# Later conditioning sections of a hybrid decoder layer: from steps in the mixer to bursts in w_o, in the second norm and in the FFN

## The chip, the core and the metric

The kernel runs on one core of one Trainium2 chip. The metric is the device time of one execution in microseconds (us); all times here are in that unit. Inputs and outputs lie in the chip's HBM in float32.

## The reference

One layer of a conditioned decoder is computed for a prompt of 256 tokens and for 8 sampled sequences of 8 tokens, 320 tokens in all, with a model width of 2048. What matters of it:

```python
mod = jax.nn.silu(c) @ w_ada + b_ada            # 9 conditioning vectors, w_ada 2048 x 12288
sh1, sc1, g1, sh2, sc2, g2 = split(mod, 6)      # sections 0 to 5, 2048 columns each
h = _rmsnorm(x, norm1_g) * (1 + sc1) + sh1
p = h @ w_in                                    # q, k, v, og, u, ga, gb, low-rank gate
y_a = norm(gated linear attention(q, k, v, state)) * silu(og)
y_b = causal pooling of u, then w_pool
x = x + g1 * ((sigmoid(ga) * y_a + sigmoid(gb) * y_b) @ w_o)
h2 = _rmsnorm(x, norm2_g) * (1 + sc2) + sh2
gate, up = split(h2 @ w_gu)                     # 2048 x 11264
x = x + g2 * ((silu(gate) * up) @ w_down)       # 5632 x 2048
y = _rmsnorm(x, final_norm_g)
```

Sections 0 and 1 of `mod` are needed at the start, section 2 (`g1`) behind the product with w_o, sections 3 and 4 (`sh2`, `sc2`) for the second norm, section 5 (`g2`) behind the product with w_down. `mod` depends on the conditioning vectors alone, so each section can be computed at any time before its use.

## The kernel before

Everything is kept transposed: a row tile is 128 of the 2048 channels by 320 tokens, and there are KT = 16 of them. A product with a weight matrix is made in units of 256 output columns (`proj`). A unit is cut into chunks of four row tiles of the weight. For each chunk a block of 128 x 4 x 256 floats, 512 KB, is loaded by SyncE's DMA queue (SP) into one of three `raw` buffers (L139). ScalarE and VectorE split it into a high and a low part, `whi` (L149) and `wlo` (L150), of which five pairs are kept. TensorE makes three matmuls for each row tile and each 128 columns (L163 to L165): 24 matmuls to a chunk, 4 chunks to a unit of a product over 2048 channels. Two PSUM buffers (`pmain`) hold the sums of such units, four smaller ones (`pmisc`) everything else.

The stages in order: the head (norms, sections 0 and 1, the first attention head's projections, to about 290 us), the mixer (attention and pooling steps of four heads, interleaved by a queue of steps with the projections of heads 1 to 3), w_o (8 units, 32 chunks), the second norm, and the FFN in two halves of 22 column tiles, each first w_gu and then w_down.

Sections 2 to 5 of `mod` are made in 16 groups of 512 columns (four row tiles of `mod`). A group needs the 16 row tiles of w_ada, 128 x 512 each. Before the change, `ada_step` (L245) does four row tiles of a group: it takes two blocks of 512 KB from a pool `ap` with AB = 3 buffers, makes 16 matmuls (L215) of the small conditioning matrix `scT` with 128 x 128 pieces of w_ada, four at a time on four column strips of the array, and asks for later blocks. Each matmul in float32 shows as two records in the profile. With the fourth step of a group, ScalarE copies the sum from PSUM (L264), TensorE transposes it (L126), and VectorE adds the bias and, for sections 1 and 4, the norm's factor (L229 to L232).

What says when a step is taken is a rate: `proj` and `projs` call `ada_pump` at the end of each chunk (L177, L191), and `ada_rate` sets how many steps come to a unit: 1.4 in the mixer (L954), 1.6 in w_o (L1004), 1.0 in the FFN (L1047). The order of the sections is 4, 2, 3, 5. Whatever of the first 48 steps is left over is done before the sixth unit of w_o is read out (L1007).

Behind a unit of w_o, `residual` (L995 to L1000) multiplies by section 2 and adds to `x1`, which holds the layer's input, loaded again from a spill in HBM (L984, 16 loads at the start of the stage). `sq_acc` collects the squares for the second norm, and GpSimd forms `xs` from the sampled tokens with section 4 (L1014). The norm then sums over channels with one matmul (`rstd_bcast`, L1022), takes root and reciprocal, and forms `h2h` and `h2l` for each row tile (L1033 to L1042), on which the FFN's matmuls wait.

The order of instructions on each engine is not that of the code. A planner orders them by the time at which its own model has each one ready, with the code's order as priority; then each engine, and SP's queue, works in order. `keep_in_program_order` pins an instruction behind the one traced before it on its engine. It is used for the first of the four matmuls of each row tile of w_ada (L217), and for loads in the head alone. Memory is given out by pools on a stack: `mix` (pools `gp` and `lp`) is closed at L980, and `fp` and `f2`, opened after it, take its place, so their first writes wait for the last reads there.

Of the kernel before, what the change touches and what calls it, by code (L numbers as in the profile page):

```python
# [11 lines left out]
F32 = mybir.dt.float32  # L12
F32R = mybir.dt.float32r
I32 = mybir.dt.int32
AF = mybir.ActivationFunctionType
# [65 lines left out]
def body(tc, A):  # L81
# [42 lines left out]
    def tr(out, in_):  # L124
        k = in_.shape[0]
        PE.transpose(out, in_, ident[:k, :k])  # L126
# [5 lines left out]
    def raw_chunk(src, nk, nn, pool=None, tag="raw", bufs=3):  # L132

        if pool is None and more:
            more.reverse()
            if more[0] is not None:
                pool, bufs = more[0], 2
        t = (pool or wp).tile([P, nk, nn], F32, tag=tag, bufs=bufs, name=nm("raw"))
        ins = nc.sync.dma_start(t, src)  # L139
        if in_order[0]:  # L140
            tc.keep_in_program_order(ins)
        return t
# [24 lines left out]
    def proj(w, col, k0, k1, xh, xl):  # L167

        ps = pmain.tile([P, 2, 512], F32, tag="pm", name=nm("ps"))
        for c0 in range(k0, k1, 4):  # L170
            nk = min(4, k1 - c0)
            for j, whi, wlo in split_chunk(w[:, c0:c0 + nk, col:col + 256], nk, 256):
                kt = c0 + j
                for i in range(2):
                    mm3(ps[:, i, :T], whi[:, i * P:(i + 1) * P], wlo[:, i * P:(i + 1) * P],
                        xh[kt], xl[kt], kt == k0, kt == k1 - 1)
            ada_pump()  # L177
        return ps

    def projs(wcols, k0, k1, xh, xl):  # L180

        pp = [pmain.tile([P, 2, 512], F32, tag="pm", name=nm("ps")) for _ in wcols]
        for c0 in range(k0, k1, 4):
            nk = min(4, k1 - c0)
            for ps, (w, col) in zip(pp, wcols):
                for j, whi, wlo in split_chunk(w[:, c0:c0 + nk, col:col + 256], nk, 256):
                    kt = c0 + j
                    for i in range(2):
                        mm3(ps[:, i, :T], whi[:, i * P:(i + 1) * P], wlo[:, i * P:(i + 1) * P],
                            xh[kt], xl[kt], kt == k0, kt == k1 - 1)  # L190
                ada_pump()  # L191
        return pp

    def proj_pair(w, col, k0, k1, xh, xl):
# [17 lines left out]
    def ada_mm(ps, k, raws, w):  # L212

        for j in range(4):
            ins = PE.matmul(ps[32 * j:32 * j + 32, 0:w], lhsT=scT[:, k, :], rhs=raws[j], start=k == 0,  # L215
                            stop=k == KT - 1, tile_position=(0, 32 * j))
            if j == 0:  # L217
                tc.keep_in_program_order(ins)

# [15 lines left out]
    ada_raw = {}  # L235
    ada_ps = []

    def ada_load(c):

        if c < 8 * len(ada_q) and c not in ada_raw:  # L240
            sec, b = ada_q[c // 8]
            col = (sec * KT + b) * P
            ada_raw[c] = raw_chunk(wada[:, 2 * (c % 8):2 * (c % 8) + 2, col:col + 512], 2, 512, apool[0], "araw", AB)

    def ada_step():  # L245

        n = len(ada_done)
        sec, b = ada_q[n // 4]
        r = n % 4
        ada_done.append(n)  # L250
        for c in range(2 * n, 2 * n + 2):
            ada_load(c)
        if r == 0:
            ada_ps[:] = [misc()]
        ps = ada_ps[0]
        for j in range(4):
            raw = ada_raw[2 * n + j // 2]
            ada_mm(ps, 4 * r + j, [raw[:, j % 2, i * P:(i + 1) * P] for i in range(4)], P)
        for c in range(2 * n + 2, 2 * n + 2 + AB):
            ada_load(c)  # L260
        if r < 3:
            return
        sb = apool[0].tile([P, P], F32, tag="adasb", name=nm("adasb"))
        S.copy(sb, ps[:, 0:P])  # L264
        pt = misc()
        tr(pt[:, 0:P], sb)
        blk = sec * KT + b
        ada_out(mod[:, blk:blk + 4, :], pt[:, 0:P].rearrange("p (m c r) -> p m c r", m=4, c=1)[:, :, :, 0:9], blk, (4, 1))

    ada_done = []  # L270
    ada_acc = [0.0, 0.0, 0]

    def ada_rate(rate, limit):

        ada_acc[:] = [0.0, rate / 4, limit]

    def ada_pump():
        ada_acc[0] += ada_acc[1]
        if ada_acc[0] >= 1.0 and len(ada_done) < ada_acc[2]:
            ada_acc[0] -= 1.0  # L280
            ada_step()

    def modp(sec, kt):
        return mod[:, sec * KT + kt, 0:1]
# [4 lines left out]
    def s3(ap):  # L289
        return ap.rearrange("p (b t) -> p b t", t=LS)  # L290
# [81 lines left out]
    with tc.tile_pool(name="head", bufs=1) as xp:  # L372
# [29 lines left out]
        class HeadJob:  # L402
# [14 lines left out]
            def burst(self, k0):  # L417
                for ahead in range(3):
                    self.load(k0 + ahead * self.nk)
                raws = self.raws[k0]  # L420
                self.raws[k0] = None
                if self.ps is None:
                    self.ps = misc()
                w = self.w
                for i in range(self.nk):
                    ada_mm(self.ps, k0 + i, [raws[j // 2][:, i, (j % 2) * w:(j % 2) * w + w] for j in range(4)], w)

            def finish(self):
                nb = self.s // 2
# [138 lines left out]
                    e += 1  # L568

    in_order[0] = False  # L570
    apool = [acx.enter_context(tc.tile_pool(name="ap", bufs=1, side="right"))]


    lp = mix.enter_context(tc.tile_pool(name="lp", bufs=1))
# [405 lines left out]
    mix.close()  # L980
    fp = ctx.enter_context(tc.tile_pool(name="fp", bufs=1))
    x1 = [fp.tile([P, T], F32, name="x1_%d" % k) for k in range(KT)]
    for k in range(KT):
        nc.sync.dma_start(x1[k], xspill[k])  # L984
    acc = fp.tile([P, T], F32, tag="acc", name="acc1")

    def sq_acc(acc, k, first):
# [13 lines left out]

    xs = fp.tile([P, KT, TS], F32, name="xs")
    tiny = fp.tile([P, 1], F32, name="tiny")
    ada_rate(1.6, 48)  # L1004
    for ui in range(8):
        ps = proj(wo, 256 * ui, 0, KT, mh, ml)
        if ui == 5:  # L1007
            while len(ada_done) < 48:
                ada_step()
        for i in range(2):  # L1010
            residual(ps, i, 2 * ui + i, 2)
            k = 2 * ui + i
            sq_acc(acc, k, k == 0)
            G.tensor_tensor(s3(xs[:, k]), s3(x1[k][:, TP:T]), mods(4, k), op=ALU.mult)  # L1014
        if ui == 4:
            ada_rate(0, 0)
        if ui == 6:
            S.activation(tiny, epst, AF.Sqrt)

    def rstd_bcast(acc):  # L1020
        pt = misc()
# [3 lines left out]
        V.reciprocal(rs, rs)  # L1025
        return rs

    f2 = ctx.enter_context(tc.tile_pool(name="f2", bufs=1))
    more[:] = [f2, None]
    rs = rstd_bcast(acc)  # L1030
    h2h = [hp.tile([P, T], F32R, tag="hh%d" % k, name="h2h%d" % k) for k in range(KT)]
    h2l = [hp.tile([P, T], F32R, tag="hl%d" % k, name="h2l%d" % k) for k in range(KT)]
    for k in range(KT):  # L1033
        t = f2.tile([P, T], F32, tag="h2", bufs=3, name=nm("h2"))
# [4 lines left out]
        S.copy(h2h[k][:, TP:T], t[:, TP:T])  # L1039
# [4 lines left out]

    acc2 = fp.tile([P, T], F32, tag="acc", name="acc2")
    parts = ((0, 22), (22, 44))
    ada_rate(1.0, 64)  # L1047
    for pi, (f0, f1) in enumerate(parts):
        ah, al = {}, {}
        for f in range(f0, f1, 2):  # L1050
            sg = f2.tile([P, 2, T], F32, tag="sg", name=nm("sg"))
            if f == 0:
                pg, pu = projs(((wgu, f * P), (wgu, FF + f * P)), 0, KT, h2h, h2l)
                S.activation(sg, pg[:, :, 0:T], AF.Silu)
            else:
                pg = proj(wgu, f * P, 0, KT, h2h, h2l)
                S.activation(sg, pg[:, :, 0:T], AF.Silu)
                pu = proj(wgu, FF + f * P, 0, KT, h2h, h2l)
            V.tensor_tensor(sg, pu[:, :, 0:T], sg, op=ALU.mult)
            th = f2.tile([P, 2, T], F32R, tag="ah%d" % ((f - f0) // 2), name=nm("ah"))  # L1060
            tl = f2.tile([P, 2, T], F32R, tag="al%d" % ((f - f0) // 2), name=nm("al"))
            hilo(th, tl, sg)
            for j in range(2):
                ah[f + j], al[f + j] = th[:, j], tl[:, j]
# [68 lines left out]
```

## Time and profile before

| what | us |
|---|---|
| median of 3 runs | 2017.34 (2016.09 to 2018.74) |
| profiled execution, its own time | 2013.89 |
| its span, first to last instruction | 2012.1 |
| TensorE (PE) busy | 1958.5 |
| VectorE (DVE) busy | 1015.4 |
| ScalarE (ACT) busy | 819.7 |

The profile is of one execution. Engines: PE is TensorE's matmuls, PEld its weight loads, DVE VectorE, ACT ScalarE, POOL GpSimd, SP SyncE, which here only issues DMAs. "L215" is a line of the kernel. A row of a timeline has the start, the time taken, engine, line, operation, output<-input, shapes and the count; in brackets stands how long the engine had been idle and what released it. Matmuls overlap, so that the distance of their starts, and not the time each one takes, tells what they cost. The clock is the share of full speed that TensorE was granted. The DMA share is that of the busy time of 16 DMA engines; it can come out a little above 1 where packets overlap.

### The profile page before, as it was taken

What the parts mean: (1) busy time and instruction counts of PE and PEld (TensorE: products, weight loads), DVE (VectorE), ACT (ScalarE), POOL (GpSimd) and SP (SyncE); (2) the same over time, 40 slices, a digit from 0 to 9 for tenths busy, and PEclk for the clock granted to TensorE, in tenths of its full rate; (3) what the DMA queues carried; (4) which work ended last, traced back from release to release, by engine and by line L of the source; (5) the groups of instructions that cost most, each with busy time, mean ns of one, the idle gap of its engine ahead of it and who ended that gap; (6) DMA issues with size and microseconds to landing.
All of it is one profiled execution on the core that took longest, in us unless ns stands there. A gap on an engine that the chain in (4) does not pass through costs nothing.

```text
span 2012.1 us, 37187 instructions
## 1 busy us (share of the span) xinstructions
PE 1958.5 (97%) x15008; PEld 1851.2 (92%) x15008; DVE 1015.4 (50%) x1881; ACT 819.7 (41%) x1466; POOL 140.0 (7%) x261
## 2 busy tenths in 40 slices
PE   7999999999999999999989999999999999999997
PEld 5889998888898899888979999999999999999997
DVE  2556665465546433665574344444444444444554
ACT  4333374354335333643344333333333343444443
POOL 1112220111001100110020000000000000000000
PEclk9999999999999999999989999999999999999998
DMA  8888755776975887569736666544444554454442
GB/s 292 287 297 272 232 158 152 251 246 193 311 242 157 275 270 229 159 222 353 233 106 217 210 201 205 172 147 150 150 152 148 153 152 147 149 155 143 150 143 90
DMA packets 319598, 400.83 MB, mean 199 GB/s; under 512 B 13529, under 2 KB 259801, under 8 KB 319089
## 3 DMA queue, kind: packets, MB, share of 16 engines
q1 hardware_dynamic: 307154, 358.21, 56.1%
q0 software_dynamic: 12272, 40.25, 5.6%
q8 instruction: 117, 1.92, 0.4%
q14 instruction: 55, 0.45, 0.1%
HBM read 373.96 MB, written 24.67 MB: 198 GB/s over the span
## 4 chain that ended last, share of the span: by engine, by line
PE 92%; DMA 4%; DVE 1%; ACT 1%; issue 1%; SPq 0%; POOL 0%; ACTq 0%; POOLq 0%; DVEq 0%
PE ps L163 27%; PE ps L164 27%; PE ps L165 27%; PE pm L215 4%; DMA raw<-w_in 2%; PE pm L126 2%; DMA raw<-w_ada 2%; PE pm L797 1%; PE pm L766 1%; PE pm L818 1%; DVE wlo L150 1%; DMA xn<-x_sample 1%; PE pm L793 0%; PE pm L755 0%; PE pm L638 0%
## 5 line engine op out<-in xcount | busy, mean ns | idle before, releaser
L150 DVE TENSOR_TENSOR wlo<-raw,whi 128x512 fp32r<-128x512 f32 x952 | 659.4, 697 | 836.1 <-ACT whi L149 825.9
L149 ACT CAST whi<-raw 128x512 fp32r<-128x512 f32 x952 | 586.8, 621 | 1016.3 <-PE ps L164 868.6
L163 PE MATMUL ps<-hh,whi 128*128 128x320 f32 x1408 | 445.9, 317 | 6.9 <-ACT whi L149 2.8
L163 PE MATMUL ps<-h2h,whi 128*128 128x320 f32 x1408 | 437.6, 311 | 5.1 <-ACT h2h L1039 5.1
L165 PE MATMUL ps<-hh,wlo 128*128 128x320 f32 x1408 | 442.3, 314 | 0.3
L164 PE MATMUL ps<-hl,whi 128*128 128x320 f32 x1408 | 440.7, 313 | 0.4 <-DVE hl L492 0.4
L164 PE MATMUL ps<-h2l,whi 128*128 128x320 f32 x1408 | 435.2, 309 | 0.0
L165 PE MATMUL ps<-h2h,wlo 128*128 128x320 f32 x1408 | 435.2, 309 | 0.0
L163 PEld LDWEIGHTS ps<-hh,whi 128*128 128x128 f32 x1408 | 266.8, 190 | 30.2 <-issue 15.3
L165 PEld LDWEIGHTS ps<-hh,wlo 128*128 128x128 f32 x1408 | 266.9, 190 | 8.4 <-issue 5.7
L163 PEld LDWEIGHTS ps<-h2h,whi 128*128 128x128 f32 x1408 | 265.3, 189 | 9.3 <-ACT h2h L1039 6.1
L164 PEld LDWEIGHTS ps<-hl,whi 128*128 128x128 f32 x1408 | 266.9, 190 | 7.1 <-issue 5.4
L164 PEld LDWEIGHTS ps<-h2l,whi 128*128 128x128 f32 x1408 | 265.3, 188 | 0.0
L165 PEld LDWEIGHTS ps<-h2h,wlo 128*128 128x128 f32 x1408 | 265.2, 188 | 0.0
L163 PE MATMUL ps<-ah,whi 128*128 128x320 f32 x704 | 217.7, 309 | 0.0
L165 PE MATMUL ps<-ah,wlo 128*128 128x320 f32 x704 | 216.5, 308 | 0.0
L164 PE MATMUL ps<-al,whi 128*128 128x320 f32 x704 | 216.5, 308 | 0.0
L164 PEld LDWEIGHTS ps<-al,whi 128*128 128x128 f32 x704 | 132.0, 187 | 0.0
L163 PEld LDWEIGHTS ps<-ah,whi 128*128 128x128 f32 x704 | 132.0, 187 | 0.0
L165 PEld LDWEIGHTS ps<-ah,wlo 128*128 128x128 f32 x704 | 131.9, 187 | 0.0
L215 PE MATMUL pm<-raw,scT 128*32 128x128 f32 (+1 forms) x2688 | 110.6, 297 | 8.1 <-DMA raw<-w_ada 8.1
L215 PEld LDWEIGHTS pm<-raw,scT 128*32 128x32 f32 x2688 | 69.9, 111 | 35.9 <-issue 20.2
(279 smaller groups left out, 1539.6 us busy)
## 6 DMA issues: line engine op xcount, KB each, us to landing
raw<-w_ada SPq DMA_DIRECT2D x192, 512.0 KB, 6.0
raw<-w_gu SPq DMA_DIRECT2D x176, 512.0 KB, 3.6
raw<-w_in SPq DMA_DIRECT2D x173, 512.0 KB, 4.2
raw<-w_down SPq DMA_DIRECT2D x80, 512.0 KB, 3.4
S<-state_gla POOLq DMA_DIRECT2D x16, 1024.0 KB, 8.4
o_gs<-S POOLq DMA_DIRECT2D x16, 1024.0 KB, 5.7
raw<-w_o SPq DMA_DIRECT2D x32, 512.0 KB, 4.8
raw<-w_down SPq DMA_DIRECT2D x16, 256.0 KB, 2.6
```

The source lines that it names most:

```text
L126: PE.transpose(out, in_, ident[:k, :k])
L149: S.copy(hi, raw)
L150: V.tensor_sub(lo, raw, hi.bitcast(F32))
L163: PE.matmul(ps, lhsT=whi, rhs=xhi, start=start, stop=False)
L164: PE.matmul(ps, lhsT=whi, rhs=xlo, start=False, stop=False)
L165: PE.matmul(ps, lhsT=wlo, rhs=xhi, start=False, stop=stop)
L215: ins = PE.matmul(ps[32 * j:32 * j + 32, 0:w], lhsT=scT[:, k, :], rhs=raws[j], start=k == 0, stop=k == KT - 1, tile_position=(0, 32 * j))
L766: PE.matmul(pt, lhsT=E["kdn"][:, s, d * P:(d + 1) * P], rhs=E["vn"][:, s], start=s == 0, stop=s == 1)
L797: PE.matmul(pt[32 * j:32 * j + 32, :], lhsT=qeP[:, d, 4 * gg + j, :], rhs=E["S0", gg, d][:, j], start=False, stop=d == 1, tile_position=(0 ...
L818: PE.matmul(pt, lhsT=kpz[:, gg, j, d * P:(d + 1) * P], rhs=E["vp"][:, gg], start=True, stop=True)
```

## The change

The rate is gone. A group is now an object: `load` fetches one of its four pieces (four row tiles of w_ada, 1 MB), `burst` makes the matmuls of whole pieces, with the last piece first, and `finish` does the copy, the transpose and the bias as before. Groups 0 to 11 (sections 2, 4 and 3 in turns) are made in w_o, each in one burst of 64 matmuls over all 16 row tiles behind the chunks named in BURSTS. Group 12 comes after the last unit of w_o, group 13 after the norm's sum; both are finished in the FFN at chunk 4. Groups 14 and 15 are made in the FFN in halves, behind chunks 16, 28, 40 and 52, with two buffers in `ap`. No such matmul is left in the mixer, and the pool `ap` of the mixer is gone.

In w_o a pool `ad` has 8 buffers of 1 MB, two groups. Each tick (the end of a chunk) asks for two loads of `x1`, one or two pieces, and reads out what is ready: a unit's `residual` waits until its group of section 2 is made, and `xs` until its group of section 4 is. The buffers `h2`, `sg` and the second set of `raw` move from `f2` to `fp`, and `f2` is opened after `ad` is closed.

```diff
-AB = 3
+AB = {"ad": 8, "ap": 2}
+BURSTS = (5, 7, 9, 12, 14, 16, 19, 21, 23, 26, 28, 30)
...
-    ada_q = [(s, b) for s in (4, 2, 3, 5) for b in range(0, KT, 4)]
...
-    def ada_step():
...
+        def load(self, p, pool):
+            col = (self.sec * KT + self.b) * P
+            self.raws[p] = raw_chunk(wada[:, 4 * p:4 * p + 4, col:col + 512], 4, 512, pool, "araw", AB[pool.name])
+
+        def burst(self, p0, p1):
+            first, last = self.ps is None, p1 == 4
+            if first:
+                self.ps = misc()
+            for p in reversed(range(p0, p1)):
+                raw = self.raws.pop(p)
+                for k in range(4):
+                    ada_mm(self.ps, 4 * p + k, [raw[:, k, i * P:(i + 1) * P] for i in range(4)], P,
+                           first and p == p1 - 1 and k == 0, last and p == p0 and k == 3)
...
-    ada_rate(1.4, 48)
     for h in range(1, H):
...
-    for k in range(KT):
-        nc.sync.dma_start(x1[k], xspill[k])
...
+    ad = adx.enter_context(tc.tile_pool(name="ad", bufs=1))
+    groups = [AdaGroup(sec, 4 * b) for sec, b in ((2, 0), (4, 0), (2, 1), (3, 0), (4, 1), (2, 2), (3, 1), (4, 2), (2, 3),
+                                                  (3, 2), (4, 3), (3, 3), (5, 0), (5, 1), (5, 2), (5, 3))]
+    nbulk = len(BURSTS) + 2
...
+    def settle():
+        while pending and have(2, 2 * pending[0][1]):
+            wo_evac(*pending.pop(0))
+        for k in [k for k in late_xs if have(4, k)]:
+            late_xs.remove(k)
+            G.tensor_tensor(s3(xs[:, k]), s3(x1[k][:, TP:T]), mods(4, k), op=ALU.mult)
+
+    def load_pieces(n):
+        for _ in range(n):
+            q = st_wo["piece"]
+            if q < 4 * nbulk and q // 4 < st_wo["burst"] + 2:
+                groups[q // 4].load(q % 4, ad)
+                st_wo["piece"] += 1
+
+    def wo_tick():
+        c = st_wo["chunk"]
+        st_wo["chunk"] += 1
+        x1_load(2)
+        n = st_wo["burst"]
+        if n < len(BURSTS) and BURSTS[n] == c:
+            groups[n].burst(0, 4)
+            st_wo["burst"] += 1
+            groups[n].finish()
+        load_pieces(1 if c < 4 else 2)
+        settle()
...
     for ui in range(8):
         ps = proj(wo, 256 * ui, 0, KT, mh, ml)
...
+        pending.append((ps, ui))
+        settle()
+    tick[0] = None
+    while st_wo["piece"] < 4 * nbulk:
+        groups[st_wo["piece"] // 4].load(st_wo["piece"] % 4, ad)
+        st_wo["piece"] += 1
+    groups[nbulk - 2].burst(0, 4)
...
+    more[:] = [fp, None]
+    rs = rstd_bcast(acc)
+    groups[nbulk - 1].burst(0, 4)
+    adx.close()
     f2 = ctx.enter_context(tc.tile_pool(name="f2", bufs=1))
...
-    ada_rate(1.0, 64)
+    def ff_tick():
...
+        if c in (16, 28, 40, 52):
+            j = (c - 16) // 12
+            g = groups[nbulk + j // 2]
+            g.burst(2 * (j % 2), 2 * (j % 2) + 2)
```

More of the change, by code (lines that the diff above doesn't have):

```diff
@@ L210, in body, with ada_mm @@
     wdn = A["w_down"][0].rearrange("(kt p) n -> p kt n", p=P)
-    def ada_mm(ps, k, raws, w):
+    def ada_mm(ps, k, raws, w, start, stop):
         for j in range(4):
-            ins = PE.matmul(ps[32 * j:32 * j + 32, 0:w], lhsT=scT[:, k, :], rhs=raws[j], start=k == 0,
-                            stop=k == KT - 1, tile_position=(0, 32 * j))
+            ins = PE.matmul(ps[32 * j:32 * j + 32, 0:w], lhsT=scT[:, k, :], rhs=raws[j], start=start,
+                            stop=stop, tile_position=(0, 32 * j))
             if j == 0:
@@ L270, in body, with __init__, finish @@
[L270 to L281, printed above, removed]
+    class AdaGroup:
+        def __init__(self, sec, b):
+            self.sec, self.b, self.ps, self.raws = sec, b, None, {}
+        def load(self, p, pool):
[10 more added lines that the diff above has]
+                           first and p == p1 - 1 and k == 0, last and p == p0 and k == 3)
+        def finish(self):
+            sb = fp.tile([P, P], F32, tag="adasb", name=nm("adasb"))
+            S.copy(sb, self.ps[:, 0:P])
+            pt = misc()
+            tr(pt[:, 0:P], sb)
+            blk = self.sec * KT + self.b
+            ada_out(mod[:, blk:blk + 4, :], pt[:, 0:P].rearrange("p (m c r) -> p m c r", m=4, c=1)[:, :, :, 0:9],
+                    blk, (4, 1))
@@ L283, in modp, with chunk_done @@
+    tick = [None]
+    def chunk_done():
+        if tick[0] is not None:
+            tick[0]()
     def modp(sec, kt):
@@ L1003, in body, with have @@
     tiny = fp.tile([P, 1], F32, name="tiny")
-    ada_rate(1.6, 48)
+    adx = ExitStack()
+    ad = adx.enter_context(tc.tile_pool(name="ad", bufs=1))
+    groups = [AdaGroup(sec, 4 * b) for sec, b in ((2, 0), (4, 0), (2, 1), (3, 0), (4, 1), (2, 2), (3, 1), (4, 2), (2, 3),
+                                                  (3, 2), (4, 3), (3, 3), (5, 0), (5, 1), (5, 2), (5, 3))]
+    nbulk = len(BURSTS) + 2
+    st_wo = dict(chunk=0, piece=0, burst=0)
+    pending = []
+    late_xs = []
+    def have(sec, b):
+        return any(g.sec == sec and g.b == b - b % 4 for g in groups[:st_wo["burst"]])
@@ new lines, in x1_load, with wo_evac @@
+    def x1_load(n):
+        for _ in range(n):
+            if st_x1:
+                k = st_x1.pop(0)
+                nc.sync.dma_start(x1[k], xspill[k])
+    def wo_evac(ps, ui):
+        for i in range(2):
+            k = 2 * ui + i
+            residual(ps, i, k, 2)
+            sq_acc(acc, k, k == 0)
+            late_xs.append(k)
+        if ui == 6:
+            S.activation(tiny, epst, AF.Sqrt)
+    def settle():
[4 more added lines that the diff above has]
+            G.tensor_tensor(s3(xs[:, k]), s3(x1[k][:, TP:T]), mods(4, k), op=ALU.mult)
@@ new lines, in load_pieces @@
+    def load_pieces(n):
+        for _ in range(n):
+            q = st_wo["piece"]
[13 more added lines that the diff above has]
+        settle()
@@ L1005, in body @@
+    st_x1 = list(range(KT))
+    x1_load(4)
+    tick[0] = wo_tick
     for ui in range(8):
         ps = proj(wo, 256 * ui, 0, KT, mh, ml)
[L1007 to L1016, printed above, removed]
@@ L1046, in body @@
     parts = ((0, 22), (22, 44))
-    ada_rate(1.0, 64)
+    st_ff = dict(chunk=0)
+    def ff_tick():
+        c = st_ff["chunk"]
+        st_ff["chunk"] += 1
+        if c == 4:
+            for g in groups[nbulk - 2:nbulk]:
+                g.finish()
+            for p in range(2):
+                groups[nbulk].load(p, ap)
+        if c in (16, 28, 40, 52):
+            j = (c - 16) // 12
+            g = groups[nbulk + j // 2]
+            g.burst(2 * (j % 2), 2 * (j % 2) + 2)
+            if j < 3:
+                for p in range(2):
+                    groups[nbulk + (j + 1) // 2].load(2 * ((j + 1) % 2) + p, ap)
+            if j % 2:
+                g.finish()
+    tick[0] = ff_tick
     for pi, (f0, f1) in enumerate(parts):
@@ L1050, in body @@
         for f in range(f0, f1, 2):
[L1051 removed]
+            sg = fp.tile([P, 2, T], F32, tag="sg", name=nm("sg"))
             if f == 0:
```

44 lines of the change are left out of this document (6 added, 38 removed).

## The prediction

> **What bounds the kernel now.** First the page: the span, the engines' totals, and the shares of the chain of work that ended last.
>
> ```profile
> span 2012.1 us, 37187 instructions
> ...
> PE 1958.5 (97%) x15008; PEld 1851.2 (92%) x15008; DVE 1015.4 (50%) x1881; ACT 819.7 (41%) x1466; POOL 140.0 (7%) x261
> ...
> PE 92%; DMA 4%; DVE 1%; ACT 1%; issue 1%; SPq 0%; POOL 0%; ACTq 0%; POOLq 0%; DVEq 0%
> ```
>
> TensorE bounds the kernel over the whole, and transfers take 4% of the chain. But that is an average, so next come the stages, by the view of busy time per window: mixer, w_o, the second norm, the first 10 us of the FFN, the rest of the FFN that holds conditioning. After the window and its length stand the busy times of PE, PEld, DVE, ACT and POOL with counts, the granted clock, the DMA share, GB/s.
>
> ```profile
> 290.00:901.00 611.00, 598.22 (x4866) 538.89 (x4868) 330.18 (x663) 267.87 (x510) 64.24 (x101) 0.99 0.70 224
> 901.00:1030.00 129.00, 128.41 (x1119) 121.31 (x1111) 69.62 (x146) 47.77 (x88) 5.01 (x14) 1.00 0.81 265
> 1030.00:1040.00 10.00, 1.77 (x3) 0.87 (x4) 7.12 (x15) 2.99 (x8) 3.08 (x9) 0.58 0.18 55
> 1040.00:1050.00 10.00, 10.00 (x53) 10.00 (x53) 9.98 (x27) 7.25 (x21) 7.89 (x18) 0.74 0.17 51
> 1050.00:1290.00 240.00, 240.00 (x2019) 233.70 (x2018) 106.06 (x164) 93.47 (x158) 4.86 (x9) 1.00 0.65 202
> ```
>
> PE is idle for 12.8 us of the mixer's 611, and the DMA engines there move 224 GB/s. w_o is already the densest long stage for transfers (265 GB/s), although it carries only a quarter of the moved conditioning. That is where I look for the answer: the change makes PE's work cheaper but crowds almost all later w_ada bytes into the shortest stage.
>
> The same windows for the conditioning matmuls alone (PE, PEld):
>
> ```profile
> 290.00:901.00 611.00, 44.23 (x1196) 30.45 (x1200) 0.99 0.70 224
> 901.00:1030.00 129.00, 13.01 (x348) 8.17 (x340) 1.00 0.81 265
> 1050.00:1290.00 240.00, 17.30 (x512) 13.00 (x512) 1.00 0.65 202
> ```
>
> A step is 16 matmuls, recorded as 32. So 1196 / 32 = 37 of the 64 steps lie in the mixer, 11 in w_o (a few records are missing), 16 in the FFN.
>
> **What a step costs PE.** The timeline of PE at the end of w_o and around one step in the FFN, and from the chain a step of 32 records and half a step of 16:
>
> ```profile
> 1023.82 0.31 PE L165 MATMUL ps<-mh,wlo 128*128 128x320 f32 x1
> ...
> 1029.10 0.31 PE L165 MATMUL ps<-mh,wlo 128*128 128x320 f32 x1
> ...
> 1071.49 0.31 PE L165 MATMUL ps<-h2h,wlo 128*128 128x320 f32 x1
> 1071.73 1.08 PE L215 MATMUL pm<-raw,scT 128*32 128x128 f32 x32
> 1072.74 0.41 PE L163 MATMUL ps<-h2h,whi 128*128 128x320 f32 x1
> 1072.99 0.31 PE L164 MATMUL ps<-h2l,whi 128*128 128x320 f32 x1
> ```
> ```profile
> 422.24 1.01 PE pm L215 x32
> ...
> 529.76 0.57 PE pm L215 x16
> ```
>
> The large matmuls start 0.147 us apart (36 intervals from 1023.82 to 1029.10). From 1071.49 to 1072.99 are 1.50 us where two such intervals would take 0.29, so a step costs 1.2 us. Sixteen more records cost 1.01 - 0.57 = 0.44 us, the rest is the price of going in and out. A burst of 128 records is then 1.01 + 6 x 0.44 + 0.2 = 3.85 us against 4 x 1.2 = 4.8; half a burst is 1.01 + 2 x 0.44 + 0.2 = 2.1.
>
> **Term 1, the mixer: -58 us.** 37 steps x 1.2 = 45. To this come waits of PE for w_ada, from the view of waits (total, times, longest):
>
> ```profile
> PE pm L215 <- DMA raw<-w_ada: 8.1, 5, 3.1
> ```
>
> 8 us, nearly all in the mixer, about 2 us at half clock behind the longest waits, and some nine transposes of a finished group with edges, 3 us together. Bounds: the steps plus all 12.8 us of idle PE plus the missing 1% of clock (6 us) give -64. If half the waits move on to w_in or the attention steps and the clock gains nothing, it is -52. The PSUM buffer that each group held while it grew is inside these bounds. ACT and DVE are busy for about half of this stage, so they can follow a denser PE.
>
> **Term 2, the FFN: -11 us.** 16 steps x 1.2 = 19.2 become four half bursts, 8.4. Their loads lie beside a stage at 202 GB/s and cost nothing; the cover would have to rise by more than half to be gone.
>
> **Term 3, w_o and the second norm: +80 us.** Now this stage runs from its first matmul to the first one of the FFN:
>
> ```profile
> 901.24 0.42 PE L163 MATMUL ps<-mh,whi 128*128 128x320 f32 x1
> ...
> 1039.63 0.90 PE L163 MATMUL ps<-h2h,whi 128*128 128x320 f32 x2 [5.13 <-ACT h2h L1039]
> ```
>
> That is 138.4 us. By PE alone the new stage is 32 chunks x 24 matmuls x 0.147 = 113 us and 12 bursts x 3.85 = 46, so 159 and the norm. But what must land first? Sizes from the list of DMA issues:
>
> ```profile
> raw<-w_ada SPq DMA_DIRECT2D x192, 512.0 KB, 6.0
> ...
> raw<-w_o SPq DMA_DIRECT2D x32, 512.0 KB, 4.8
> ...
> x<-xspill SPq DMA_DIRECT2D x16, 160.0 KB, 4.8
> ```
>
> A group is 8 loads of 512 KB, 4.19 MB (now 4 pieces of 1 MB). Twelve groups and the two of the norm are 58.7 MB. When can they start? The piece buffers lie where the mixer's buffers lay, and the new pool waits for the old ones. SP's timeline, then DVE's:
>
> ```profile
> 886.44 11.14 SPq L139 DMA_DIRECT2D raw<-w_o  x3
> ...
> 901.96 1.40 SPq L139 DMA_DIRECT2D raw<-w_o  x1
> ...
> 914.60 0.42 SPq L139 DMA_DIRECT2D raw<-w_o  x1
> 915.11 2.09 SPq L984 DMA_DIRECT2D x<-xspill  x4
> ```
> ```profile
> 911.95 0.49 DVE L933 TENSOR_TENSOR mg<-EQK,mg 128x320 f32<-128x320 f32 x1
> ...
> 913.36 1.30 DVE L297 TENSOR_TENSOR ml<-mg,mh 128x320 fp32r<-128x320 f32 x3
> ```
>
> The first load into that space left 0.5 us behind the last read of the mixer's buffers, 14 us after w_o had begun (the `ml` of three row tiles, from `merged`). The attention buffers, under the pieces, are last read by the merge at 911.95, so I take 13 us for the pieces. By then 7 of 32 w_o chunks are loaded; 25 remain, 13.1 MB, and x1, 2.6 MB. Together 74.4 MB. The rate, from busy windows:
>
> ```profile
> 105.00:115.00 10.00, 9.64 (x64) 9.08 (x63) 9.93 (x24) 5.73 (x13) 7.46 (x16) 1.00 1.06 399
> 513.00:525.00 12.00, 9.88 (x122) 8.95 (x112) 9.91 (x19) 2.49 (x4) 0.53 (x2) 1.00 1.03 375
> 905.00:955.00 50.00, 50.00 (x483) 44.90 (x482) 26.68 (x60) 17.04 (x33) 2.24 (x4) 1.00 1.05 356
> ```
>
> With the engines full (share above 1.0) they moved 356 to 399 GB/s. The rows do not tell what each window's mixture was; the last one is a w_o stage with w_ada and x1, as the new one will be, but with less w_ada. I take 380, nearest to the middle row. Then 74.4 / 0.380 = 196 us. The stage is 13 + 196 + 2 (landing) + 4 (the last burst) = 215, and 4 us for holes in the stream make 219: 219 - 138.4 = +80. The 16 us that bursts save on PE, and the norm's gap in which two of them lie, are worth nothing in a stage that waits for bytes. At 399 GB/s without holes it is 205 us (+67), at 356 with 10 us of holes 238 (+100).
>
> Waits that the change adds: a burst waits for its fourth piece, and behind it on PE stand its transpose and the next w_o chunks; the pieces of group n+2 wait on SP for burst n, and the next w_o loads stand behind them; `residual` waits for its group of section 2, and with two PSUM buffers for w_o the third unit waits for burst 0. In a stream that stays full these waits cost nothing more, since group n+1 (11 us of transfer) is still under way while burst n runs. `x1` and `xs` are needed no earlier than before.
>
> The Trainium skill, DMA: Bandwidth & Descriptors, section Bandwidth, has 425 GB/s for 16 MB on a lone core, and about 358 GB/s per core where both of a pair stream. By 425 the transfers would take an estimated 175 us and the kernel 2005, by 358 an estimated 208 and 2038. The 399 of this trace, with one core at work, speaks against a cap of 358; no window reaches 425, so neither figure has a chance of its own.
>
> **Term 4, the clock: -2 us.** After the norm's gap the large matmuls start 0.267 us apart:
>
> ```profile
> 1040.87 0.47 PE L163 MATMUL ps<-h2h,whi 128*128 128x320 f32 x1
> 1041.13 0.47 PE L164 MATMUL ps<-h2l,whi 128*128 128x320 f32 x1
> ```
>
> The window 1040 to 1050 holds 53 matmuls where 68 fit: 2.2 us that a burst right before may save. Bounds 0 and -2.5.
>
> **Sum.** -58 - 11 + 80 - 2 = +9 on the profiled execution, which took 2013.89 us around its span of 2012.1. The median of the runs shown, 2017.34, is 3.45 above it, so 2013.9 + 9 + 3.4 = **2026 us**.
>
> **The rivals.** *Pieces come early.* If the new buffers come free one by one, the first eight pieces (8.4 MB, 22 us of transfer) can ride on the mixer's last 25 us, which have room:
>
> ```profile
> 880.00:890.00 10.00, 10.00 (x70) 8.82 (x68) 6.36 (x16) 6.59 (x14) 0.56 (x1) 1.00 0.39 132
> 890.00:900.00 10.00, 10.00 (x72) 9.37 (x74) 10.00 (x18) 5.26 (x11) 2.67 (x2) 1.00 0.60 205
> ```
> ```profile
> 900.12 0.80 POOL L822 DMA_DIRECT2D o_gs<-S  x1 [1.50 <-DVE S L820]
> ```
>
> The stage loses some 20 us: +9 - 20 = -11, 2006 us. It decides for faster from about 13 us of earlier start. For it: the last state left its buffer at 900.12. Against it: x1 left all together behind the last read. *The high rate.* 399 GB/s, no holes, the mixer at -60: -60 - 11 + 67 - 2 = -6, 2011; with 390 GB/s 2016. So it straddles no change. *Holes.* If SP's order makes w_o loads stand behind pieces that wait for a burst while nothing else is under way, each of the 12 rounds leaves the engines empty for about 2 us, half a burst: +24 on top, 2050. For it: one queue, in order, for all loads. Against it: two groups of buffers. *The change does not do what it says:* only the first matmul of each row tile is pinned behind its predecessors, so the planner may split bursts; 36 edges more at 0.33 us are 12 us of PE, hidden in a stage that waits for transfers. It stays within the forecast.
>
> **Chances and range.** Forecast (2018 to 2034) 0.43; early pieces 0.19; high rate 0.20; holes (2034 to 2055) 0.18. A measurement of this kernel tells about 0.2%, 4 us, from no change. Faster: 0.19 and half of 0.20, less a little, 0.28. Same: 0.11 of the high rate and 0.08 of the forecast's lower end, 0.19. Slower: 0.35 of the forecast and 0.18, 0.53. The range, **2006 to 2044**, leaves out half of the early pieces and the upper half of the holes; the forecast alone has 2018 to 2034.
>
> **What would show it.** In the profile after, the mixer should be about 555 us at some 190 GB/s with no conditioning matmuls. w_o and the norm should take 205 to 235 us with a DMA share near 1.0 and 370 to 390 GB/s, and PE should wait there for raw<-w_ada or for casts that wait for raw<-w_o. The first piece should leave within 2 us of the last merge. The FFN to the end should be about 11 to 13 us shorter. Wrong would be the step on the transfers if the share in w_o stays below 0.9 while PE is full, or if pieces leave before the last merge; wrong would be term 1 if the mixer shrinks by less than 52 us.

## The result and the profile after

The changed kernel took 2029.54 us (median of 4 runs, 2028.82 to 2030.01), the kernel before, on the same chip, 2016.71 (4 runs, 2014.64 to 2018.74). The ratio is 1.0063 with an interval of 1.0046 to 1.0081: slower by 0.6%. The forecast was 2026 us, slower, in a range of 2006 to 2044. The profiled execution took 2030.01 us around a span of 2028.2, so 16.1 us more than before by the spans, where the sum had +9.

The page of the kernel after: span, engines' totals, shares of the chain that ended last.

```profile
span 2028.2 us, 37056 instructions
...
PE 1943.5 (96%) x15008; PEld 1859.5 (92%) x15008; DVE 1012.9 (50%) x1881; ACT 821.8 (41%) x1469; POOL 137.7 (7%) x261
...
PE 89%; DMA 7%; DVE 2%; SPq 1%; ACT 1%; issue 0%; ACTq 0%; DVEq 0%
```

TensorE has 15 us less to do than before and the kernel takes 16 us longer. In the chain, transfers go from 4% to 7%. Where this happens is told by the first large matmul of each stage. The timeline of PE in the kernel after (start, length, operation, in brackets the idle time before it and what ended it):

```profile
835.85 0.41 PE L164 MATMUL ps<-mh,whi 128*128 128x320 f32 x1 [0.77 <-DVE mg L911]
...
886.29 1.29 PE L216 MATMUL pm<-raw,scT 128*32 128x128 f32 x20 [16.89 <-DMA raw<-w_ada]
...
1063.72 5.22 PE L216 MATMUL pm<-raw,scT 128*32 128x128 f32 x128 [7.63 <-DMA raw<-w_ada]
1068.87 0.41 PE L164 MATMUL ps<-h2h,whi 128*128 128x320 f32 x1
```

| stage | before | after | measured | forecast |
|---|---|---|---|---|
| start to the first w_o matmul | 901.24 | 835.85 | -65.4 | -58 |
| w_o and the second norm | 138.4 | 233.0 | +94.6 | +80 |
| first FFN matmul to the end of the span | 972.5 | 959.3 | -13.1 | -11 - 2 |
| span | 2012.1 | 2028.2 | +16.1 | +9 |

Busy time per window of the kernel after, in the columns of the prediction's first such view: the mixer, w_o with the norm, the same from the first piece on, the first 10 us of the FFN.

```profile
283.00:836.00 553.00, 549.45 (x3692) 509.64 (x3692) 329.72 (x653) 271.99 (x509) 65.75 (x101) 0.99 0.57 179
836.00:1069.00 233.00, 184.05 (x2575) 174.55 (x2576) 85.90 (x194) 56.24 (x120) 14.14 (x38) 0.90 0.99 349
850.00:1064.00 214.00, 165.05 (x2360) 155.75 (x2362) 66.90 (x155) 47.29 (x100) 9.58 (x28) 0.90 1.03 365
1069.00:1079.00 10.00, 10.00 (x69) 10.00 (x70) 10.00 (x26) 7.18 (x18) 4.48 (x11) 1.00 0.69 231
```

The mixer is 553 us long at 179 GB/s, nearly without idle time. In w_o PE is idle for 49 of 233 us while the DMA share is 0.99: the stage has turned from one that PE fills into one that waits for bytes. The FFN's first 10 us run at full clock, with 69 matmul records where before had 53.

The view of transfers in the window from 836 to 1069 us: the busy share of the DMA engines in tenths and the rate in 40 slices of 5.8 us, then the issues with their sizes and the median time to landing.

```profile
DMA  6769997999999999999999999999999999999970
GB/s 241 252 214 397 384 367 233 308 366 366 387 381 374 380 384 381 372 378 371 383 378 371 381 377 378 379 380 378 377 378 371 368 384 368 380 382 377 377 256 10
...
raw<-w_ada SPq DMA_DIRECT2D x56, 1024.0 KB, 13.2
raw<-w_o SPq DMA_DIRECT2D x28, 512.0 KB, 12.1
raw<-w_gu SPq DMA_DIRECT2D x7, 512.0 KB, 11.8
x<-xspill SPq DMA_DIRECT2D x16, 160.0 KB, 5.7
```

All 56 pieces go through this stage. From the ninth slice on the rate hardly moves for 30 slices, 366 to 387 GB/s. Before that is a dip to 233 at 871 to 877 us, where the engines are busy for only seven tenths. And seven chunks of w_gu, for the FFN, are loaded in this stage, all but the last of them issued ahead of the last two pieces.

What stands at the start of the stage shows the queue of SP and the merge on DVE, timelines of the kernel after:

```profile
824.68 23.41 SPq L140 DMA_DIRECT2D raw<-w_o  x6
850.04 7.73 SPq L140 DMA_DIRECT2D raw<-w_ada  x6
857.88 17.43 SPq L1004 DMA_DIRECT2D x<-xspill  x16
875.36 0.98 SPq L140 DMA_DIRECT2D raw<-w_ada  x2
876.39 6.55 SPq L140 DMA_DIRECT2D raw<-w_o  x3
```
```profile
849.02 0.88 DVE L920 TENSOR_TENSOR mg<-EQK,mg 128x320 f32<-128x320 f32 x2
```

The merge ends by 849.9, the first piece leaves at 850.04. Eight pieces and sixteen loads of x1 then stand ahead of the next w_o load, which leaves at 876.39. PE's wait of 16.89 us before 886.29 lies there (that row ends where the view ends; the burst has 128 records and took 5.19 us). It is the second burst, and what it waited for was its last pieces, which left at 875.36, behind x1. The next w_o chunk was no earlier: its cast began at 887.78, so PE would have stood without that burst too.

The loads of x1 take SP 17.43 / 16 = 1.1 us each, which for 160 KB is 150 GB/s: the dip falls where the six pieces issued before them have run out. The view of SP's own waits in this stage puts part of the 17.43 us down to landings of pieces:

```profile
SPq L1004 <- DMA raw<-w_ada: 5.8, 3, 2.4
```

### The profile page after: what moved, and what is told of

Its sections match the earlier page's. It is cut to its first block, busy times and chain, and to the rows that moved or that the text cites. A ratio compares the mean times of both kernels' runs of the same rounds, so it can differ in the third digit from the quotient of the medians.

```text
span 2028.2 us, 37056 instructions
## 1 busy us (share of the span) xinstructions
PE 1943.5 (96%) x15008; PEld 1859.5 (92%) x15008; DVE 1012.9 (50%) x1881; ACT 821.8 (41%) x1469; POOL 137.7 (7%) x261
## 4 chain that ended last, share of the span: by engine, by line
PE 89%; DMA 7%; DVE 2%; SPq 1%; ACT 1%; issue 0%; ACTq 0%; DVEq 0%
PE ps L164 26%; PE ps L166 26%; PE ps L165 26%; PE pm L216 3%; DMA raw<-w_o 3%; DMA raw<-w_ada 2%; PE pm L127 2%; DMA raw<-w_in 1%; SPq L140 1%; PE pm L784 1%; PE pm L753 1%; PE pm L805 1%; DMA x<-xspill 1%; DVE wlo L151 1%; DMA xn<-x_sample 1%
## 5 line engine op out<-in xcount | busy, mean ns | idle before, releaser
L164 PE MATMUL ps<-hh,whi 128*128 128x320 f32 x1408 | 441.2, 314 | 6.3 <-ACT whi L150 2.8
L216 PE MATMUL pm<-raw,scT 128*32 128x128 f32 (+1 forms) x2688 | 101.2, 305 | 34.6 <-DMA raw<-w_ada 34.6
L216 PEld LDWEIGHTS pm<-raw,scT 128*32 128x32 f32 x2688 | 78.8, 117 | 48.7 <-issue 24.4
```

Source lines behind the costliest of these rows:

```text
L164: PE.matmul(ps, lhsT=whi, rhs=xhi, start=start, stop=False)
```

## The experiments

Each run is compared with the kernel before on its own chip; n is the number of runs. Stage lengths are from the first w_o matmul to the first FFN matmul.

**1. Half of the bytes.** From the changed kernel:

```
 def load(self, p, pool):
+    if p >= 2 and pool.name == "ad":
+        self.raws[p] = self.raws[p - 2]
+        return
```

> Each of the 14 groups made in w_o and the norm loads two of its four pieces and uses each twice (so those parts of the conditioning are computed from the wrong half of w_ada): 29.4 MB less, all matmuls kept. Transfers bound the stage: 78 MB become 49 MB, 130 us at 375 GB/s, so PE with 113 us of w_o and 46 us of bursts takes over; the stage falls from 233 us to 165 to 180, the kernel to about 1965 to 1980 us. Bursts and their order on PE bound it: the stage stays near 225, the kernel near 2025.

1985.60 us (n = 2), ratio 0.9863 (0.9844 to 0.9883). The window of w_o and the norm:

```profile
833.00:1025.00 192.00, 173.83 (x2575) 166.26 (x2574) 79.96 (x172) 52.78 (x103) 7.67 (x22) 0.96 0.80 271
```

Same matmuls, 192 us instead of 233. The bytes set the length of the change's stage. The 165 to 180 us that were expected were not reached, nor was the kernel's time: PE is still idle for 18 us, nearly all of it before 904, where w_o's loads stand behind pieces and x1.

**2. A quarter of the conditioning matmuls.** From the changed kernel:

```
-    for k in range(4):
+    for k in range(1):
...
```

> All pieces are loaded, but of each only one row tile of four is multiplied (conditioning incomplete): a burst is 16 matmuls in place of 64, about 1.2 us in place of 3.85, some 35 us of PE less in w_o and the norm and 5 in the FFN. Transfers bound the stage: it stays at 225 to 233 us and the kernel loses the FFN's 5 us and up to 4 of the last burst, 2018 to 2026. PE bounds it: the stage falls to about 200, the kernel to about 1990.

2013.91 us (n = 8), ratio 1.0000 (0.9988 to 1.0012), some 4 us below what transfers alone had let expect.

```profile
836.00:1056.00 220.00, 145.63 (x1198) 135.04 (x1198) 78.99 (x173) 51.39 (x105) 8.81 (x22) 0.83 1.02 360
```

With 38 us less on PE the stage is 13 us shorter, the share stays at 1.02 and PE's idle time grows from 49 to 74 us. So PE is the lesser limit. How much of the 13 us it is worth cannot be read from this run alone, since one thing confounds it: the last burst came to stand behind the first FFN matmuls, so that the FFN no longer waited for it. Experiment 11 takes that alone.

**3. Only the norm and the FFN part.** The 48 steps of before stay in mixer and w_o; section 5 goes as in the change:

```
-BURSTS = (5, 7, 9, 12, 14, 16, 19, 21, 23, 26, 28, 30)
+BURSTS = ()
...
+    ada_q = [(s, b) for s in (4, 2, 3) for b in range(0, KT, 4)]
...
+    ada_rate(1.4, 48)
...
+    ada_rate(1.6, 48)
```

> The steps of sections 4, 2 and 3 stay in the mixer and w_o as before the change; only section 5 is changed, two bursts around the norm's sum and two groups in halves in the FFN. The prediction's terms 2 and 4: FFN shorter by 11 to 14 us, w_o takes 8.4 MB more at 265 GB/s and has room, so about 2004 (-13, ratio 0.9935). If the pieces crowd w_o, its stage grows by up to 10 us and the kernel stays within 0.2% of before.

2024.74 us (n = 4), ratio 1.0058 (1.0043 to 1.0073): slower, where 2004 was expected. The rest from the first FFN matmul on was as short as in the change, but w_o with the norm took 161 us. Its window, 20 us of it, and the view of PE's waits in this stage:

```profile
905.00:1066.00 161.00, 139.37 (x1366) 130.97 (x1365) 76.54 (x157) 49.93 (x95) 6.52 (x21) 0.93 0.77 258
940.00:960.00 20.00, 4.35 (x27) 3.63 (x28) 2.83 (x5) 2.90 (x5) 0.00 (x0) 0.50 1.05 368
```
```profile
PE ps L165 <- ACT whi L151: 15.4, 1, 15.4
```

One hole of 15.4 us, while the DMA engines are full (1.05): they carry the pieces for the norm and x1, and w_o's own load stands behind them (none leaves SP from 915.86 to 943.22).

**4. Eight groups in the mixer, four bursts in w_o.** Sections 2 and 4 as 32 steps in the mixer, section 3 as four bursts, section 5 as in the change:

```
+BURSTS = (13, 18, 23, 28)
...
+    ada_q = [(s, b) for s in (2, 4) for b in range(0, KT, 4)]
...
+    ada_rate(1.2, 32)
```

> Sections 2 and 4 go back into the mixer as 32 steps, section 3 is four bursts in w_o, section 5 as in the change. Transfers: w_o and the norm have 45 MB from 14 us on, 120 us at 375 GB/s, so 134, and PE 113 + 15 + norm: the stage is near the 138 of before; the mixer has 5 steps less than before (-6), the FFN -13: about 1998 to 2004, faster than both kernels. If bursts and waits bound w_o by themselves, a third of the 95 us that the change cost there stays, and it is above 2020.

2014.05 us (n = 10), ratio 1.0001 (0.9990 to 1.0011), again above what was expected. Window of the stage, the timeline of PE around the hole, SP's timeline:

```profile
888.00:1051.00 163.00, 139.40 (x1542) 136.02 (x1541) 75.86 (x159) 49.77 (x93) 8.05 (x20) 0.93 0.86 291
```
```profile
915.70 0.31 PE L167 MATMUL ps<-mh,wlo 128*128 128x320 f32 x1
...
938.99 0.63 PE L165 MATMUL ps<-mh,whi 128*128 128x320 f32 x1 [22.98 <-ACT whi L151]
```
```profile
900.04 10.48 SPq L141 DMA_DIRECT2D raw<-w_ada  x6
910.64 15.64 SPq L1057 DMA_DIRECT2D x<-xspill  x16
926.32 0.98 SPq L141 DMA_DIRECT2D raw<-w_ada  x2
927.35 6.08 SPq L141 DMA_DIRECT2D raw<-w_o  x3
```

23 us without a matmul, and the order of SP tells why: from 900.04 to 927.35 no w_o load leaves. Bytes are not short here over the whole (291 GB/s); the wrong ones come first.

**5. The same work, another order.** From experiment 4: x1 is loaded first, and each piece is kept behind the w_o load of its chunk, one per chunk from the eighth on.

```
-        if in_order[0]:
+        if in_order[0] or (pool is not None and pool.name == "ad"):
...
-        x1_load(2)
...
-        load_pieces(1 if c < 4 else 2)
+        load_pieces(1 if c >= 7 else 0)
...
-    x1_load(4)
+    x1_load(KT)
```

The bursts stand behind chunks 13, 17, 21 and 26.

> As the kernel with sections 2 and 4 in the mixer, but x1 is loaded ahead of the pieces, and each piece stands in SP's queue behind the w_o load of its chunk, one to a chunk from the eighth on; bursts behind chunks 13, 17, 21 and 26. If the 23 us in which PE waited there for casts came from w_o loads that stood behind eight pieces and x1 in one queue, most of it goes: 1992 to 2000 us. If it came from too many bytes in the stage, it stays, 2010 to 2016.

1999.93 us (n = 4), ratio 0.9926 (0.9906 to 0.9946): faster than both kernels. The window of the stage and SP's timeline:

```profile
888.00:1039.00 151.00, 140.87 (x1543) 136.96 (x1541) 75.86 (x159) 48.53 (x94) 6.38 (x21) 0.97 0.93 315
```
```profile
903.93 13.68 SPq L1057 DMA_DIRECT2D x<-xspill  x16
917.71 0.38 SPq L141 DMA_DIRECT2D raw<-w_o  x1
918.14 0.51 SPq L141 DMA_DIRECT2D raw<-w_ada  x1
918.74 0.52 SPq L141 DMA_DIRECT2D raw<-w_o  x1
```

Same matmuls, same bytes, 12 us less in this stage (PE idle for 10 us instead of 24).

**6. Experiment 3 with that order**, one piece in every second chunk from the thirteenth on:

```
-        load_pieces(1 if c < 4 else 2)
+        load_pieces(c % 2 if c >= 12 else 0)
```

> As the kernel that changes section 5 alone, but the eight pieces follow w_o's loads one by one from its twelfth chunk, and x1 comes first. Queue order: the hole of 16 us behind the pieces closes and the FFN's 13 us show, about 2002 to 2008. Bytes: the stage stays 23 us longer than before, 2024.

2001.75 us (n = 6), ratio 0.9944 (0.9923 to 0.9964), 23 us below experiment 3:

```profile
901.00:1041.00 140.00, 137.33 (x1367) 128.46 (x1367) 75.40 (x159) 49.14 (x95) 8.36 (x22) 1.00 0.89 298
```

The hole is gone: PE is busy for 137 of 140 us.

**7. w_gu behind the pieces.** From the changed kernel, the FFN's first eight w_gu loads are held behind all pieces:

```
+                in_order[0] = True
                 pg, pu = projs(((wgu, f * P), (wgu, FF + f * P)), 0, KT, h2h, h2l)
+                in_order[0] = False
```

> The changed kernel with the FFN's first eight w_gu loads held behind all pieces on SP. The seven w_gu loads that ran ahead of the last pieces are 3.7 MB, 10 us at 378 GB/s: if the stage ends when the last piece lands, the last burst starts up to 10 us sooner, and since the first w_gu chunk then lands some 3 us behind it, the kernel gains 4 to 8 us, 2019 to 2025. If these loads filled time in which the queue waited for buffers, nothing changes or it gets slower.

2029.15 us (n = 4), ratio 1.0069 (1.0049 to 1.0090): the time of the changed kernel, without the 4 to 8 us that were expected. The window from the first piece on, then PE's timeline:

```profile
850.00:1060.00 210.00, 167.89 (x2478) 158.65 (x2476) 66.79 (x160) 46.24 (x101) 13.11 (x34) 0.90 1.04 367
```

```profile
1053.11 5.24 PE L216 MATMUL pm<-raw,scT 128*32 128x128 f32 x128 [4.55 <-DMA raw<-w_ada]
...
1064.63 0.63 PE L164 MATMUL ps<-h2h,whi 128*128 128x320 f32 x1 [3.33 <-ACT whi L150]
```

The last burst starts at 1053.11 instead of 1063.72, 10.6 us sooner, as the bytes of the held chunks let expect. But the FFN starts only at 1064.63, some 6 us behind the burst, when the first w_gu chunk has been cast. That chunk had landed near 1054.4 (issued at 1041.3, 13.1 us to landing); its cast stands on ScalarE behind the making of most of `h2h` and begins at 1063.97. The stage got 4 us shorter, and the FFN took 3 of them back. So the order of the loads moved the last burst, and the order on ScalarE kept the kernel from gaining by it.

**8. The steps of before without their loads.** From the kernel before; sections 2 to 4 are computed from the first three blocks, which stay in their buffers:

```
 def ada_load(c):
+    if 3 <= c < 96:
+        ada_raw[c] = ada_raw[c % 3]
+        return
```

> The kernel before, with its 48 steps in the mixer and w_o unchanged on PE, but all of them on the first three blocks loaded (sections 2 to 4 are computed from wrong columns of w_ada): 48 MB less. The mixer lost 65 us by the change where the prediction had 58. If 8 us of waits and a slow clock behind them (some 90 matmul intervals at 0.267 in place of 0.147 us, 11 us) are the rest beside 37 steps, this kernel is 15 to 22 us faster than before, 1992 to 1999, and its mixer about 600 us. If the steps themselves cost more than 1.2 us, it is only 8 to 10 us faster.

1996.39 us (n = 2), ratio 0.9907 (0.9876 to 0.9938). The window of the mixer, all engines and then the conditioning matmuls alone:

```profile
290.00:890.00 600.00, 593.40 (x4945) 540.45 (x4947) 333.17 (x668) 267.71 (x510) 64.63 (x101) 0.99 0.52 166
```
```profile
290.00:890.00 600.00, 43.39 (x1276) 33.59 (x1280) 0.99 0.52 166
```

w_o begins near 890, 11 us earlier than before, although 1280 / 32 = 40 steps now lie in the mixer instead of 37 or 38. From here to the 835.85 of the change are 54 us for 40 steps, 1.35 us each with what belongs to their groups.

**9. Ten groups in the mixer**, two bursts in w_o behind chunks 20 and 25, pieces from the thirteenth chunk on, order as in experiment 5. Of the edit against experiment 5, the line of the bursts:

```
-BURSTS = (13, 17, 21, 26)
+BURSTS = (20, 25)
```

> Ten groups (sections 2, 4 and half of 3) as 40 steps in the mixer, two bursts in w_o behind chunks 20 and 25, section 5 as in the change, pieces one by one behind w_o's loads from the twelfth chunk on. The stage carries 8.4 MB less than with eight groups in the mixer, 37 MB from 14 us on, 98 us at 375 GB/s, so PE bounds it: about 138 to 142 us in place of 152 (-11), and the eight steps more in the mixer cost 1.2 to 1.6 us each (+10 to +13). So 1996 to 2003 us. If the holes at the start of w_o cost as much here, 2005 and more.

2000.74 us (n = 4), ratio 0.9927 (0.9899 to 0.9954). No difference to experiment 5: its w_o begins 17.8 us later (905.44 instead of 887.69), and w_o with the norm is 17.7 us shorter (133.9 instead of 151.6). With the order right, it matters little whether eight or ten groups go through the mixer.

**10. Buffers for one group.** From the changed kernel:

```
-AB = {"ad": 8, "ap": 2}
+AB = {"ad": 4, "ap": 2}
...
-            if q < 4 * nbulk and q // 4 < st_wo["burst"] + 2:
+            if q < 4 * nbulk and q // 4 < st_wo["burst"] + 1:
```

and the last group's loads behind the burst of the one before it.

> The changed kernel with four piece buffers in place of eight: the next group's pieces leave only behind the burst before. If two groups of buffers are what keeps the transfer engines full (share 1.06 in w_o), they now run empty in each round while a burst runs and its successor's first piece is on its way, some 2 to 4 us in 13 rounds: 2055 to 2080 us. If the stream is kept full by w_o's own loads, it stays at 2025 to 2035.

2076.90 us (n = 2), ratio 1.0304 (1.0263 to 1.0345). Window and PE's waits in the stage:

```profile
850.00:1100.00 250.00, 166.29 (x2305) 159.20 (x2308) 61.50 (x143) 45.17 (x89) 4.67 (x16) 0.85 0.88 306
```
```profile
PE pm L216 <- DMA raw<-w_ada: 69.2, 11, 16.1
```

The share falls to 0.88: now bursts wait eleven times, 69.2 us in all, for loads that could only leave behind the burst before. This is the rival of holes, made real. By the spans it costs 50 us, 39 of them in the stage and 11 in the FFN, where the prediction had priced 24; what makes up the FFN's part was not divided. Two groups of buffers keep it out of the change.

**11. The last burst in the FFN.** From the changed kernel, group 13's burst stands behind the FFN's fifth chunk:

```
-    groups[nbulk - 1].burst(0, 4)
-    adx.close()
...
         if c == 4:
+            groups[nbulk - 1].burst(0, 4)
+            adx.close()
```

> The changed kernel with one edit: the burst of the last bulk group (group 13) and the closing of its buffers stand behind the fifth chunk of the FFN instead of behind the sum of the second norm; loads and everything else stay. In the changed kernel TensorE waited 7.6 us for that group's last piece and then ran the burst for 5.2 us, and the first FFN matmul started behind it. Theory (the FFN's start waits for that piece and not for w_gu, as the run with a quarter of the matmuls suggests): w_o with the norm shrinks from 233 us to 219-222 us, the burst costs 3.6-4 us in the FFN and the FFN starts at a lower clock again (2 us), so 2018-2023 us, a ratio to the kernel before of 1.001 to 1.005. Rival (the bytes are needed for the FFN's start anyway, w_gu's chunks or the next loads stand behind the pieces): the FFN starts early and then waits for w_gu by about the same time, 2027-2031 us.

2028.47 us (n = 7), ratio 1.0048 (1.0033 to 1.0062), not told apart from the change. PE's timeline:

```profile
1060.24 0.90 PE L164 MATMUL ps<-h2h,whi 128*128 128x320 f32 x2 [5.13 <-ACT h2h L1073]
...
1080.81 3.70 PE L216 MATMUL pm<-raw,scT 128*32 128x128 f32 x128
```

The FFN starts 8.6 us earlier, and from its first matmul to the end it takes 2027.0 - 1060.24 = 966.8 us instead of 959.3. It gives 7.5 back: 3.7 are the burst, and the start after a gap of 5.13 us is at the lower clock again (two matmuls in 0.90 us). The theory named both and expected more to be left; what makes up the rest was not divided. The time lies in the rival's range, but its mechanism, a wait for w_gu, does not show in PE's waits. Experiment 2 has its last burst in the FFN too, so this run is what to compare it with. From here, the quarter of the matmuls takes 30.5 us off PE's busy time in the stage, and the stage is 4.8 us shorter (219.7 instead of 224.5); from the first FFN matmul to the end it is 9.8 us shorter (957.0 instead of 966.8), where the bursts are cheaper as well. So of the 13 us that experiment 2 took off the stage, some 8.5 came with the move of the last burst, and the FFN gives nearly all of these back, and about 5 came from PE's cheaper bursts.

## Why the prediction was right, and where its terms were off

**The sign and the mechanism held.** w_o waits for bytes: half of the pieces' bytes took 41 us off the stage, and with seven w_gu chunks held back the last burst starts 10.6 us sooner. The forecast's signs came: share near 1.0, PE waiting for raw<-w_ada, the first piece 0.2 us behind the last merge. One of them missed: the rate, 349 GB/s over the whole stage and 365 from the first piece on, instead of 370 to 390. That PE's work is worth nothing in this stage was nearly so: 30.5 us less of it gave 4.8 (experiment 2 against 11).

**Term 3 was too small by 15 us**, +94.6 instead of +80. The wait for the buffers was 14.2 us (forecast 13). From 850.04 until the last burst could start at 1063.72 are 213.7 us, in which 214 x 0.365 = 78.1 MB moved. The step had 74.4 MB; the difference, 3.7 MB, is the seven w_gu chunks of the FFN, which it did not count, and which cost 3.7 / 0.380 = 10 us (experiment 7 bears that out). The rate was 365 instead of 380, 78.1 / 0.365 - 78.1 / 0.380 = 8.5 us more. The slices place that: after the dip they stay near 378, close to what was chosen; the loss is in the dip (233 and 308) and at both ends (214 and 256). The last burst took 5.2 us instead of 4. Against this, 2 us of landing and 4 us of holes were counted apart, but lie in the 213.7: 1.2 + 10 + 8.5 + 1.2 - 6 = 15.

**Term 1 was too small by 7 us**, -65.4, one more than its bound of -64. Experiment 8 divides it: 11 us come from the loads, 54 from the steps. By its 1.35 us a step, the 37.5 steps of before (1200 / 32) took 51 us, where the prediction had 48 with transposes; then 14 us remain for waits and clock, where it had 10. The 1.2 us had been read from one unbroken step in the FFN.

**Terms 2 and 4** were right together: -13.1 against -13. No run divides them.

So two misses of opposite sign, +15 and -7, made a sum that is 7 us off; that they had opposite signs is luck. On the medians the change cost 12.8 us and not 16, since the kernel before was profiled 2.8 us under its median and the one after 0.5 over. The median, 2029.54, so came nearer to the forecast of 2026 than the sum deserved.

**The rivals.** Early pieces: fell, the pool came free as a whole at 850.04. The high rate: fell with 365. Holes: not as a steady loss, since two groups of buffers held, but once, at the start, where w_o loads stood behind pieces and x1, and the second burst's last pieces behind x1: 16.9 us of idle PE before 886.29. In the change bytes set the end anyway, which hid it. In experiments 3 and 4, with few bytes, it was the whole difference between slower or no change, and 0.6% to 0.7% faster. I had weighed this rule of order for pieces that wait for a burst; it struck earlier, with pieces that had nothing to wait for. *The change does not do what it says* did not come: all steps left the mixer, and the timeline has each of the 14 bursts whole, 128 records in a row.

**The better version.** Experiment 5 and the kernel before differ so: the mixer ends 13 us earlier, near 888 (32 steps instead of 37 or 38, which at 1.35 us explains about half), w_o and the norm are 13 us longer, and the FFN to the end of the span at 1998.0 is 13.7 us shorter. The gain of moving work out of the mixer is eaten by w_o in it too; what is left is the FFN's. Experiments 6 and 9 come to the same 2001 us with little or nothing moved out of the mixer.

## What to carry to other kernels

When work moves, its bytes move: divide the bytes that must land in the new stage, with the next stage's prefetch counted in, by the rate of a full stretch, and compare it with the stage's PE time before anything else. Where bytes fit, look at the order in the issuing queue: large loads that are needed late, put as soon as buffers are free, delay small ones that are needed now, and here x1 first and then one piece behind each urgent load cured it (the two were not tried apart). A stage with both limits near each other gives back only part of what is taken off one of them.

## What the runs showed of the hardware

The full stream was steadier than expected: 366 to 387 GB/s in 30 slices, some 175 us, where the w_o window before had 356. The Trainium skill, DMA: Bandwidth & Descriptors, section Bandwidth, has 425 GB/s for one core and about 358 for each when two stream. This core, alone, lay between them. The dip to 233 follows x1's sixteen loads of 160 KB, issued in 17.4 us; whether their pace on SP, their size or their shape is the cause was not isolated, and the slice of 308, with nearly full engines, stays unexplained.

A burst's length depends on the wait before it. From the chain of the kernel after, a burst without one:

```profile
941.06 3.63 PE pm L216 x128
```

Behind the waits of 16.89 and 7.63 us, and behind one of 4.31 us at 1049.96, the same 128 records took 5.19, 5.22 and 5.40 us, the first part of them at a granted clock of 0.50. The Trainium skill, TensorE: Matmul & The Clock Gate, section Part 1, says that the array's clock is halved after an idle window of about 3.4 us. The trace agrees with that for these three waits. It does not for a shorter one: the burst at 920.03, behind a wait of 2.12 us, took 5.37 us, at a clock of 0.50 from 921 to 923, while the burst at 904.72, behind 2.36 us, took 3.70. So here a wait shorter than the page's window cost a burst as much, once in two.
